# Two last output projections by token tile, with kept weights, and other row statistics

## The chip, the cores and the metric

The kernel runs on 1 core of one Trainium2 chip. The metric is the device time of one execution in microseconds; the time before is 2203.59 us, the median of 3 runs (2201.79 to 2204.91).

## The reference

An encoder trunk of two layers on 512 tokens of width 2048, all float32. Each layer is a mixer with one input projection and one output projection, followed by a residual sum and a layer norm:

```python
for i in range(DEPTH):                          # DEPTH = 2, ALPHA = 4 ** 0.25
    y = attention_mixer(x, ...) if i % 2 == 0 else retention_mixer(x, ...)
    x = layer_norm(ALPHA * x + y, ln_gain[i], ln_bias[i])
```

Layer 0 is grouped-query attention (16 heads of 128 in 4 groups, normalised q and k, rotary positions), its result times a SiLU gate, times `w_out` (2048 x 2048). Layer 1 is retention (8 heads, q and k of 256, v of 512, two directions with decay), each head normalised, times a SiLU gate, times `w_out` (4096 x 2048). `layer_norm` takes mean and variance over the 2048 columns of a token, then gain and bias. Only the second layer norm's result is the output.

## The kernel before, in words

**Numbers.** A float32 product is made of three fp32r matmuls: each operand is split into a high part (a cast on ScalarE, L104) and a low part (a subtraction on VectorE, L105), and `mm3` (L220 to L222) adds high x high, high x low, low x high in one PSUM bank of 128 x 512. So one "product" is three matmuls of 128 x 128 weights and 512 columns.

**Tiles.** The 512 tokens are 4 token tiles of 128 (`t`), the 2048 output columns 4 column blocks of 512 (`c`). Weights come in chunks of 128 x 1024 (512 KB), two pieces of 128 rows x 512 columns each. One list, `order`, holds every chunk of the whole kernel in the order of use; `next_chunk` hands out the next one, has the chunks two further on split (`AHEAD`), and has loads issued three chunks beyond (`FETCH`). Raw chunks lie in pool `rp` (9 buffers), split ones in `wp` (3 buffers each of `whi` and `wlo`). Pool `xp` has 32 buffers of 128 x 1024 (`x4`), used for operands, sums, attention and retention pieces; `tmp` 13 of 128 x 512; PSUM 8 banks.

**Input projections** take one Strassen-like step: seven products (`ORDER`) per block of weights, each with its own "form" of the transposed activations (`Operand.form`), that is a sum or difference of quarters `x11`, `x12`, `x21`, `x22`, split into high and low. Forms 1 and 2 are the quarters of the first two token tiles themselves. `FORMS` says at which chunk of which block's product a form is made; both layers use it.

**Output projections** (`Sum.out_proj`) run once per group of heads, spread between the units of the next group by a `Stream` whose `pump(us)` puts so many us of matmuls (0.68 per product) into PE's order; they add to the residual sum `y` in SBUF (`Sum.add`). The last one of a layer (`out_proj_last`) has no attention or retention beside it. It runs by pairs of token tiles: for the pair `r` = 0, then 2, all four column blocks, so each weight chunk is loaded and split twice (`outs[-1].add(1)` puts a second pass into `order`). After each add, `bn_stats` takes the row statistics of the 512 columns.

**Between the layers**, once a pair of tiles is done, `norm_1` normalises them in place (without gain and bias) and stores them to `nD`; `turn_1` transposes a tile's column block on PE (4 transposes of 128 x 128 into one bank) and writes four pieces of 128 x 128 with gain and bias, two on ScalarE, two on VectorE; for the first pair each is also split at once (128 x 512). Form 5 follows the second pair's turns, and then the hooks make the others.

**At the end**, `norm_2` makes mean and 1 / deviation of a tile (the power on GpSimd, L414), and for each column block subtracts, multiplies by the gain (L926), multiplies by 1 / deviation and adds the bias (L931) on VectorE; the last columns go by ScalarE (L939) and GpSimd (L940, L941). 16 stores go out on SyncE.

**Order.** PE's order is the program's, by hand (`manual_schedule`). The other engines' instructions, DMA queues too, are put in order by a planner that goes by priority (earlier in the program first) among what it holds to be ready and to have a buffer; each engine then runs its list in order.

## Time and profile before

| | |
|---|---|
| median of 3 runs | 2203.59 us |
| profiled execution | 2198.51 us |
| its span | 2196.6 us |
| PE, VectorE, ScalarE, GpSimd busy | 98%, 72%, 48%, 16% |
| mean granted TensorE clock | 0.992 |
| DMA, mean | 165 GB/s |

The span runs from the first to the last instruction; the execution's own time has 1.9 us around it. PE is the matmul engine, PEld its weight load, DVE is VectorE, ACT ScalarE, POOL GpSimd, SP SyncE; SPq is SyncE's queue of DMA issues. The ends of matmuls are modelled: 0.39 us is written for a matmul of 512 columns where the next starts 0.227 us after it. A granted clock of 1.00 is 2.4 GHz.

### The profile page before, as it was taken

Reading aid. Unit: us, or ns where it says so; the run is one execution under the profiler, and the core shown is the slowest. Engines: PE = TensorE matmul, PEld = TensorE weight load, DVE = VectorE, ACT = ScalarE, POOL = GpSimd, SP = SyncE. Lnnn points to the kernel's source line nnn. Section 1 sums busy time; section 2 is a strip of 40 time slices with the busy share of each in tenths; the row PEclk is TensorE's granted clock in tenths of the full one; section 3 lists DMA queues with packets and bytes.
Section 4 is the critical chain, followed back from the end, with each engine's and each line's share of the span. In section 5 each row is a group of like instructions: output and inputs, shape, how many; then the busy total and the mean of one; then the engine's idle time right before and its main releaser. Section 6 shows DMA issues by size and latency. Waiting matters only on the chain.

```text
span 2196.6 us, 26556 instructions
## 1 busy us (share of the span) xinstructions
PE 2142.0 (98%) x9888; PEld 1767.6 (80%) x9888; DVE 1586.9 (72%) x2189; ACT 1043.4 (48%) x1365; POOL 341.5 (16%) x391
## 2 busy tenths in 40 slices
PE   8999999999999999999999999999999999999994
PEld 6778788888888778878888888888888888888883
DVE  6766978887778986767786676657677666666668
ACT  5545446754455654444444444444465333333332
POOL 0322434000000121211212111111111000000004
PEclk9999999999999999999999999999999999999997
DMA  9976666543215688686777558566667433343342
GB/s 337 211 195 133 169 173 148 184 177 106 95 60 171 207 189 220 163 244 177 176 198 210 132 142 213 155 130 183 178 162 262 160 117 107 122 135 125 101 139 77
DMA packets 111600, 361.42 MB, mean 165 GB/s; under 512 B 13680, under 2 KB 17008, under 8 KB 111472
## 3 DMA queue, kind: packets, MB, share of 16 engines
q1 hardware_dynamic: 76272, 235.99, 32.4%
q0 software_dynamic: 35200, 123.75, 25.7%
q8 instruction: 77, 1.26, 0.2%
q14 instruction: 51, 0.42, 0.1%
HBM read 311.45 MB, written 48.23 MB: 164 GB/s over the span
## 4 chain that ended last, share of the span: by engine, by line
PE 82%; DVE 7%; DMA 4%; issue 3%; POOL 2%; ACT 1%; SPq 0%; POOLq 0%; ACTq 0%; DVEq 0%
PE acc L221 23%; PE acc L222 23%; PE acc L220 23%; PE tr L431 3%; DVE wlo L105 3%; DMA raw<-in_wa_in_dram 2%; PE o L220 2%; PE o L222 2%; PE o L221 2%; DMA raw<-in_wr_in_dram 2%; PE s L220 1%; PE s L222 1%; PE s L221 1%; ACT whi L104 1%; DVE f L105 1%
## 5 line engine op out<-in xcount | busy, mean ns | idle before, releaser
L105 DVE TENSOR_TENSOR wlo<-raw,whi 128x1024 fp32r<-128x1024 f32 (+1 forms) x589 | 716.9, 1221 | 362.2 <-ACT whi L104 355.4
L104 ACT CAST whi<-raw 128x1024 fp32r<-128x1024 f32 (+1 forms) x589 | 618.8, 1052 | 744.2 <-PE acc L222 651.4
L220 PE MATMUL acc<-whi,f 128*128 128x512 f32 x1904 | 750.5, 394 | 9.3 <-ACT f L104 4.5
L221 PE MATMUL acc<-wlo,f 128*128 128x512 f32 x1904 | 745.0, 391 | 6.6 <-DVE wlo L105 6.4
L222 PE MATMUL acc<-whi,f 128*128 128x512 f32 x1904 | 743.8, 391 | 0.7 <-DVE f L105 0.7
L221 PEld LDWEIGHTS acc<-wlo,f 128*128 128x128 f32 x1904 | 358.7, 188 | 85.3 <-DVE wlo L105 13.4
L220 PEld LDWEIGHTS acc<-whi,f 128*128 128x128 f32 x1904 | 358.6, 188 | 83.9 <-ACT whi L104 5.2
L222 PEld LDWEIGHTS acc<-whi,f 128*128 128x128 f32 x1904 | 358.3, 188 | 76.7 <-DVE f L105 1.6
L221 PE MATMUL acc<-wlo,ogh 128*128 128x512 f32 x768 | 301.3, 392 | 11.5 <-DVE wlo L105 11.5
L220 PE MATMUL acc<-whi,ogh 128*128 128x512 f32 x768 | 306.0, 398 | 0.5 <-ACT p L604 0.5
L222 PE MATMUL acc<-whi,ogl 128*128 128x512 f32 x768 | 301.0, 392 | 0.0
L221 PEld LDWEIGHTS acc<-wlo,ogh 128*128 128x128 f32 x768 | 145.5, 189 | 40.5 <-DVE wlo L105 12.7
L222 PEld LDWEIGHTS acc<-whi,ogl 128*128 128x128 f32 x768 | 145.2, 189 | 31.1
L220 PEld LDWEIGHTS acc<-whi,ogh 128*128 128x128 f32 x768 | 145.1, 189 | 28.7 <-ACT p L604 0.9
L116 POOL DMA_DIRECT2D raw<-in_wr_in_dram x104 | 91.7, 882 | 384.0 <-DVE wlo L105 246.7
L365 DVE TENSOR_TENSOR y<-acc,y 128x512 f32<-128x512 f32 x176 | 115.6, 684 | 18.7 <-PE acc L222 18.7
L414 POOL TENSOR_TENSOR rstd<-rs_e,neg_half 128x1 f32<-128x1 f32 x40 | 23.8, 597 | 674.4 <-DVE rs_e L413 674.4
L154 DVE TENSOR_TENSOR raw<-raw,raw 128x1024 f32<-128x1024 f32 x52 | 63.5, 1223 | 35.9 <-DMA raw<-in_wr_in_dram 30.9
L152 DVE TENSOR_TENSOR raw<-raw,raw 128x1024 f32<-128x1024 f32 x68 | 82.1, 1218 | 0.8
L328 ACT COPY t<-acc 128x512 f32<-128x512 f32 x102 | 59.0, 587 | 41.9 <-PE acc L222 38.0
L867 ACT ACTIVATE o<-o,nmr,rstd 128x512 f32<-128x512 f32 x32 | 24.9, 779 | 93.4 <-DVE nmr L425 93.4
L604 ACT ACTIVATE p<-s,nmax,q_rs 128x512 f32<-128x512 f32 x64 | 50.0, 781 | 30.6 <-DVE nmax L602 28.2
(159 smaller groups left out, 2098.8 us busy)
## 6 DMA issues: line engine op xcount, KB each, us to landing
raw<-in_wr_in_dram SPq DMA_DIRECT2D x152, 512.0 KB, 4.8
raw<-in_wr_in_dram POOLq DMA_DIRECT2D x104, 512.0 KB, 6.1
raw<-in_wr_o_dram SPq DMA_DIRECT2D x72, 512.0 KB, 3.5
raw<-in_wa_in_dram SPq DMA_DIRECT2D x67, 512.0 KB, 5.1
raw<-in_wa_in_dram POOLq DMA_DIRECT2D x48, 512.0 KB, 6.4
raw<-in_wa_o_dram SPq DMA_DIRECT2D x40, 512.0 KB, 3.5
qkD<-qkT POOLq DMA_DIRECT2D x32, 256.0 KB, 4.4
vDr<-t POOLq DMA_DIRECT2D x32, 256.0 KB, 5.4
```

The source lines that it names most:

```text
L104: nc.scalar.copy(hi, src)
L105: nc.vector.tensor_sub(lo, src, hi.bitcast(F32))
L116: nc.gpsimd.dma_start(out=x, in_=src, accum_op=ALU.add)
L152: nc.vector.tensor_add(v, v, g[3, c])
L154: nc.vector.tensor_add(v, v, g[2, c])
L220: nc.tensor.matmul(ps, sh, mh, start=start, stop=False, skip_group_check=go_on)
L221: nc.tensor.matmul(ps, sh, ml, start=False, stop=False, skip_group_check=go_on)
L222: nc.tensor.matmul(ps, sl, mh, start=False, stop=stop, skip_group_check=go_on)
L328: nc.scalar.copy(keep[p, t], bk[CHAIN[p]][t])
L365: nc.vector.tensor_add(y, ps, y)
L431: nc.tensor.transpose(out=b[:, tcols(i)], in_=src[:, tcols(i)], identity=ident)
L604: nc.scalar.activation(pt, sb, AF.Exp, scale=rs, bias=nmax, accum_out=self.sm[:, h:h + 1])
```

## The change

Both last output projections: the first `A_KEEP` = 2 (attention) or `R_KEEP` = 0 (retention) column blocks go over all four token tiles as in `out_proj`; the others go token tile by token tile, with the split weights of these blocks kept in pool `xp` (8 and 16 buffers), taken up at the first tile. The second pass over the weights is no longer in `order`. Statistics stay `bn_stats` in the first layer (`quick`); in the second the last add also gives a row sum, and ScalarE's squares of the centred row give the variance. `norm_1` and `norm_2` run for each tile. `turn_1` now takes two blocks of 128 columns for both tiles of a pair, transposes four times into one bank and writes two pieces of 128 x 256, one on ScalarE and one on VectorE; forms 1 and 2 are split whole (128 x 1024). Form 7 is made in `x11` instead of `x22`, and forms 3, 7 and 4 are made later, for both layers. `norm_2` is all VectorE but for the squares, with the centred rows in buffers of their own.

```diff
--- before.py
+++ after.py
@@ -33,6 +33,7 @@
 FETCH = 3
 MM3 = 0.68
 LOOK = 2
+A_KEEP, R_KEEP = 2, 0
 ORDER = (1, 5, 6, 3, 7, 2, 4)
 CHAIN = {1: "x", 6: "x", 7: "x", 4: "x", 5: "y", 3: "y", 2: "z"}
@@ -169,16 +170,17 @@
     class Plain:
-        def __init__(self, w):
-            self.w, self.got = w, {}
-        def add(self, half=0):
+        def __init__(self, w, keep=4):
+            self.w, self.got, self.keep = w, {}, keep
+        def add(self):
             for c in range(4):
                 for kc in range(2):
-                    order.append((self, (half, c), kc))
-        def fetch(self, p, kc):
-            self.got[p, kc] = raw_load(self.w[p[1], kc])
+                    order.append((self, c, kc))
+        def fetch(self, c, kc):
+            self.got[c, kc] = raw_load(self.w[c, kc])
         def make(self, p, kc):
             return self.got.pop((p, kc))
@@ -198,7 +200,10 @@
     def make_chunk():
         blk, p, c = order[len(ready)]
         raw = blk.make(p, c)
-        hi, lo = [wp.tile([P, CH], F32R, tag=n, name=nm(n)) for n in ("whi", "wlo")]
+        if isinstance(blk, Plain) and p >= blk.keep:
+            hi, lo = x4("wkh"), x4("wkl")
+        else:
+            hi, lo = [wp.tile([P, CH], F32R, tag=n, name=nm(n)) for n in ("whi", "wlo")]
         split(hi, lo, raw)
         blk.follow(p, c)
         ready.append([(half(hi, j), half(lo, j)) for j in range(2)])
@@ -268,9 +273,9 @@
             elif n == 3:
                 nc.vector.tensor_add(x12, x12, x11)
             elif n == 7:
-                nc.vector.scalar_tensor_tensor(out=x22, in0=x11, scalar=-1.0, in1=x22,
+                nc.vector.scalar_tensor_tensor(out=x11, in0=x11, scalar=-1.0, in1=x22,
                                                op0=ALU.mult, op1=ALU.subtract)
-            split(*self.new_form(n, i), {1: x11, 2: x12, 5: x21, 6: x11, 4: x22, 3: x12, 7: x22}[n])
+            split(*self.new_form(n, i), {1: x11, 2: x12, 5: x21, 6: x11, 4: x22, 3: x12, 7: x11}[n])
         def st(self, n, k, t):
             return [m[:, k % 4, tcols(t)] for m in self.f[n, k // 4]]
@@ -345,8 +350,9 @@
     class Sum:
-        def __init__(self):
-            self.y, self.st, self.rows = {}, {}, []
+        def __init__(self, quick=()):
+            self.y, self.st, self.rows, self.quick = {}, {}, [], quick
         def load(self, src):
             for t in range(NT):
@@ -357,16 +363,23 @@
                         self.y[t, 2 * i + j] = half(m, j)
                     self.y[t, "pair", i] = m
-        def add(self, t, c, ps, scale):
+        def add(self, t, c, ps, scale, last=False):
             y = self.y[t, c]
-            if scale != 1.0:
+            if last and t not in self.st:
+                self.st[t] = small("ln_st", 24)
+            if last and t not in self.quick:
+                nc.vector.scalar_tensor_tensor(out=y, in0=y, scalar=scale, in1=ps, op0=ALU.mult, op1=ALU.add,
+                                               accum_out=self.st[t][:, c:c + 1])
+            elif scale != 1.0:
                 nc.vector.scalar_tensor_tensor(out=y, in0=y, scalar=scale, in1=ps, op0=ALU.mult, op1=ALU.add)
             else:
                 nc.vector.tensor_add(y, ps, y)
-        def out_proj(self, og, scale):
-            for c in range(4):
+            if last and t in self.quick:
+                nc.vector.bn_stats(self.st[t][:, 6 * c:6 * c + 6], y)
+        def out_proj(self, og, scale, cols=(0, 1, 2, 3), last=False):
+            for c in cols:
                 banks = {}
                 for kc in range(2):
                     ks = next_chunk()
@@ -379,28 +392,36 @@
                             mm3(banks[t], og(k, t), ks[kk], k == 0, k == 3)
                             yield MM3
                 for t in range(NT):
-                    self.add(t, c, banks[t], scale)
-        def out_proj_last(self, og):
...
-                self.rows.append(r)
+                    self.add(t, c, banks[t], scale, last)
+        def mean_rstd(self, t):
+            if t in self.quick:
+                return mean_rstd(self.st[t])
+            mu, neg, sq, rstd = small("k_rs", 4)[:, 0:1], small("nmr"), small("sm", 4), small("rstd")
+            nc.vector.tensor_reduce(out=mu, in_=self.st[t][:, :4], axis=AX.X, op=ALU.add)
+            nc.vector.tensor_scalar_mul(neg, mu, -1.0 / D)
+            nc.vector.tensor_scalar_mul(mu, mu, 1.0 / D)
+            for c in range(4):
+                nc.scalar.activation(temp("sq"), self.y[t, c], AF.Square, bias=neg, accum_out=sq[:, c:c + 1])
+            nc.vector.tensor_reduce(out=neg, in_=sq, axis=AX.X, op=ALU.add)
+            rsqrt(rstd, neg, 1.0 / D, LN_EPS)
+            return mu, rstd
+        def out_proj_last(self, og, keep):
+            yield from self.out_proj(og, 1.0, range(keep), True)
+            ws = {}
+            for t in range(NT):
+                for c in range(keep, 4):
+                    b = bank()
+                    for k in range(4):
+                        if t == 0 and k % 2 == 0:
+                            ws[c, k // 2] = next_chunk()
+                        mm3(b, og(k, t), ws[c, k // 2][k % 2], k == 0, k == 3)
+                        yield MM3
+                    self.add(t, c, b, 1.0, True)
+                self.rows.append(t)
     ident = const.tile([P, P], F32, name="ident")
@@ -434,8 +455,8 @@
     a_in = [Block(a["wa_in"][g], g < 2) for g in range(A_G)]
     r_in = [Block(a["wr_in"][g], g < 2) for g in range(R_G)]
-    a_out = [Plain(a["wa_o"][g]) for g in range(GROUPS)]
-    r_out = [Plain(a["wr_o"][h]) for h in range(R_HEADS)]
+    a_out = [Plain(a["wa_o"][g], A_KEEP if g == GROUPS - 1 else 4) for g in range(GROUPS)]
+    r_out = [Plain(a["wr_o"][h], R_KEEP if h == R_HEADS - 1 else 4) for h in range(R_HEADS)]
     for ins, outs in ((a_in, a_out), (r_in, r_out)):
         for b in ins[:2]:
             b.add((1, 2))
@@ -445,7 +466,6 @@
             b.add(ORDER)
         for b in outs:
             b.add()
-        outs[-1].add(1)
     def in_stream(ins, op, evacuate, n):
@@ -456,8 +476,8 @@
         for b in ins[2:len(ins) - n]:
             yield from products(b, op, ORDER, evacuate)
-    FORMS = (((1, 2, 1), (6, 0)), ((1, 2, 3), (6, 1)), ((0, 5, 0), (4, 0)), ((0, 5, 1), (4, 1)),
-             ((0, 5, 2), (3, 0)), ((0, 5, 3), (3, 1)), ((0, 6, 0), (7, 0)), ((0, 6, 1), (7, 1)))
+    FORMS = (((1, 2, 1), (6, 0)), ((1, 2, 3), (6, 1)), ((0, 5, 1), (3, 0)), ((0, 5, 3), (3, 1)),
+             ((0, 3, 0), (7, 0)), ((0, 3, 2), (7, 1)), ((0, 7, 0), (4, 0)), ((0, 7, 2), (4, 1)))
     def form_hooks(ins, op):
         for (b, p, c), what in FORMS:
@@ -671,7 +691,7 @@
     ev1 = spill(deliver_1)
     Stream(in_stream(a_in, x1, ev1, 1)).drain()
     groups = [Group(g) for g in range(GROUPS)]
-    total = Sum()
+    total = Sum(range(NT))
     work = Stream(products(a_in[-1], x1, ORDER, ev1))
     work.pump(31.5 * MM3)
     groups[0].load_kv()
@@ -724,7 +744,7 @@
     x2 = Operand()
     def norm_1(t):
-        mu, rstd = mean_rstd(total.st[t])
+        mu, rstd = total.mean_rstd(t)
         scale, shift = scale_shift(mu, rstd)
         for c in (0, 2, 1, 3):
             y = total.y[t, c]
@@ -735,22 +755,24 @@
         for i in range(2):
             nc.gpsimd.dma_start(out=nD[:, t, i * 1024:i * 1024 + 1024], in_=total.y[t, "pair", i])
-    def turn_1(t, c):
-        b = transpose4(total.y[t, c])
...
-                                     scale=lnt[:, 0, k:k + 1], bias=lnt[:, 1, k:k + 1])
+    def turn_1(r, m):
+        b = bank("tr")
+        kh, i = m // 4, m // 2 % 2
+        for k in (2 * m, 2 * m + 1):
+            for t in range(2):
+                nc.tensor.transpose(out=b[:, tcols(k % 2 * 2 + t)],
+                                    in_=total.y[2 * r + t, k // 4][:, tcols(k % 4)], identity=ident)
+        for k in (2 * m, 2 * m + 1):
+            o = 256 * (k % 2)
+            f = x2.quarter(r, kh, i)[:, k % 4]
+            if k % 2:
+                nc.vector.tensor_scalar(f, b[:, o:o + 256], lnt[:, 0, k:k + 1], lnt[:, 1, k:k + 1],
+                                        op0=ALU.mult, op1=ALU.add)
             else:
-                nc.vector.tensor_scalar(f[:, j], b[:, tcols(j)], lnt[:, 0, k:k + 1], lnt[:, 1, k:k + 1],
-                                        op0=ALU.mult, op1=ALU.add)
-        if r == 0:
-            if (1 + kh, i) not in x2.f:
-                x2.new_form(1 + kh, i)
-            split(*[m[:, :, cols] for m in x2.f[1 + kh, i]], f)
+                nc.scalar.activation(f, b[:, o:o + 256], AF.Identity, scale=lnt[:, 0, k:k + 1], bias=lnt[:, 1, k:k + 1])
+        if r == 0 and m % 2:
+            x2.form(1 + kh, i)
     def residual_2(c, t, gb={}):
@@ -916,56 +938,29 @@
                 lnp[-1] += [half(u, j) for j in range(2)]
     def norm_2(t):
-        mu, rstd = mean_rstd(total.st[t])
-        def store(c):
-            nc.sync.dma_start(out=out[t, :, c * 512:c * 512 + 512], in_=total.y[t, c])
-        def centre(c):
+        mu, rstd = total.mean_rstd(t)
+        z = [half(m, j) for m in (x4("z", F32), x4("z", F32)) for j in range(2)] if t > 1 else [temp("z") for _ in range(4)]
+        for c in range(4):
             y = total.y[t, c]
-            return nc.vector.scalar_tensor_tensor(out=y, in0=y, scalar=mu, in1=lnp[0][c],
-                                                  op0=ALU.subtract, op1=ALU.mult)
-        def finish(c):
+            nc.vector.scalar_tensor_tensor(out=z[c], in0=y, scalar=mu, in1=lnp[0][c], op0=ALU.subtract, op1=ALU.mult)
+        for c in range(4):
             y = total.y[t, c]
-            nc.vector.scalar_tensor_tensor(out=y, in0=y, scalar=rstd, in1=lnp[1][c], op0=ALU.mult, op1=ALU.add)
-            store(c)
...
-            finish(c)
+            nc.vector.scalar_tensor_tensor(out=y, in0=z[c], scalar=rstd, in1=lnp[1][c], op0=ALU.mult, op1=ALU.add)
+            nc.sync.dma_start(out=out[t, :, c * 512:c * 512 + 512], in_=y)
     ev2 = spill(deliver_2)
-    work = Stream(total.out_proj_last(groups[-1].out), in_stream(r_in, x2, ev2, 1))
-    work.until(lambda: 0 in total.rows)
...
-        x2.form(5, h)
+    work = Stream(total.out_proj_last(groups[-1].out, A_KEEP), in_stream(r_in, x2, ev2, 1))
+    for r in range(2):
+        for t in (2 * r, 2 * r + 1):
+            work.until(lambda: t in total.rows)
+            norm_1(t)
+        work.pump(13.0 if r else 5.0)
+        for m in (0, 1, 4, 5, 2, 3, 6, 7) if r else range(8):
+            turn_1(r, m)
+            work.pump(2.2 if r else 0.8)
+            if r and m in (5, 7):
+                x2.form(5, m // 2 % 2)
     form_hooks(r_in, x2)
     work.drain()
@@ -983,15 +978,12 @@
         work.drain()
         if h == 0:
             total.load(lambda t: yD2[:, t])
-    work = Stream(total.out_proj_last(heads[-1].out))
-    work.pump(20.0)
+    work = Stream(total.out_proj_last(heads[-1].out, R_KEEP))
+    work.pump(5.0)
     ln_params()
-    work.until(lambda: 0 in total.rows)
-    norm_2(0)
-    norm_2(1)
-    work.drain()
-    norm_2(2)
-    norm_2(3)
+    for t in range(NT):
+        work.until(lambda: t in total.rows)
+        norm_2(t)
```

## Rows read from the trace of the kernel before

**Rows 1.** The page's first line and PE's busy time (share of the span, instructions).

```profile
span 2196.6 us, 26556 instructions
PE 2142.0 (98%) x9888; PEld 1767.6 (80%) x9888; DVE 1586.9 (72%) x2189; ACT 1043.4 (48%) x1365; POOL 341.5 (16%) x391
```

**Rows 2.** The timeline of PE in the last output projection: start, duration, engine, line, operation, output and inputs, and in brackets the idle time before and what ended it.

```profile
2151.91 0.39 PE L220 MATMUL acc<-whi,ogh 128*128 128x512 f32 x1
2160.78 0.80 PE L221 MATMUL acc<-wlo,ogh 128*128 128x512 f32 x1 [8.48 <-DVE wlo L105]
...
2165.18 0.40 PE L222 MATMUL acc<-whi,ogl 128*128 128x512 f32 x1
```

**Rows 3.** The timelines of PE and of VectorE at the end, the last row of each.

```profile
2176.55 0.39 PE L222 MATMUL acc<-whi,ogl 128*128 128x512 f32 x1
...
2192.63 0.75 DVE L931 SCALAR_TENSOR_TENSOR y<-y,rstd,ln_bias 128x512 f32<-128x512 f32 x1
```

**Rows 4.** The timeline of PE between the layers.

```profile
716.88 0.39 PE L220 MATMUL acc<-whi,ogh 128*128 128x512 f32 x1
720.09 0.50 PE L221 MATMUL acc<-wlo,ogh 128*128 128x512 f32 x1 [2.83 <-DVE wlo L105]
...
724.79 0.39 PE L222 MATMUL acc<-whi,ogl 128*128 128x512 f32 x1
...
734.80 0.66 PE L431 MATMUL tr<-ident,y 128*128 128x128 f32 x4 [1.24 <-DVE y L732]
...
794.71 0.50 PE L220 MATMUL acc<-whi,f 128*128 128x512 f32 x1 [0.32 <-ACT whi L104]
796.98 0.50 PE L221 MATMUL acc<-wlo,f 128*128 128x512 f32 x1 [1.77 <-DVE wlo L105]
```

**Rows 5.** The timeline of PE in the first layer's input projection.

```profile
76.32 0.39 PE L220 MATMUL acc<-whi,f 128*128 128x512 f32 x1
78.01 0.50 PE L221 MATMUL acc<-wlo,f 128*128 128x512 f32 x1 [1.31 <-DVE wlo L105]
```

**Rows 6.** Busy time of each engine in stretches (start:end and length, then PE, PEld, DVE, ACT, POOL with instructions in brackets, granted clock, DMA share, GB/s).

```profile
55.00:79.00 24.00, 22.69 (x100) 18.50 (x99) 23.57 (x22) 15.39 (x17) 5.35 (x7) 1.00 0.88 193
...
699.00:728.00 29.00, 25.99 (x121) 20.35 (x120) 28.10 (x54) 20.78 (x36) 3.66 (x6) 0.94 0.53 187
728.00:775.00 47.00, 45.76 (x222) 37.65 (x221) 45.04 (x71) 32.94 (x48) 8.83 (x12) 1.00 0.87 260
775.00:800.00 25.00, 22.91 (x104) 18.57 (x103) 25.00 (x32) 12.67 (x16) 5.56 (x7) 1.00 0.56 126
800.00:830.00 30.00, 29.63 (x131) 24.22 (x130) 18.28 (x18) 13.37 (x14) 8.79 (x12) 1.00 1.01 242
...
2161.30:2164.70 3.40, 3.40 (x9) 2.67 (x8) 3.40 (x5) 0.00 (x0) 2.16 (x2) 0.50 0.09 33
```

**Rows 7.** The timelines of VectorE and GpSimd around that stop of PE, in order of time.

```profile
2148.64 0.74 DVE L931 SCALAR_TENSOR_TENSOR y<-y,rstd,ln_bias 128x512 f32<-128x512 f32 x1
2149.30 0.74 DVE L926 SCALAR_TENSOR_TENSOR y<-y,mv,ln_gain 128x512 f32<-128x512 f32 x1
...
2152.85 1.71 POOL L940 TENSOR_TENSOR y<-y,ln_gain 128x512 f32<-128x512 f32 x1
2154.52 0.54 POOL L414 TENSOR_TENSOR rstd<-rs_e,neg_half 128x1 f32<-128x1 f32 x1
2155.09 0.21 DVE L425 TENSOR_SCALAR nmr<-mv,rstd 128x1 f32<-128x1 f32 x1 [1.66 <-POOL rstd L414]
...
2158.44 2.28 DVE L105 TENSOR_TENSOR wlo<-raw,whi 128x1024 fp32r<-128x1024 f32 x1
```

**Rows 8.** Groups of instructions by line and shape on VectorE and ScalarE, over the whole run: busy us and mean ns of one, then the idle time before them and what ended it.

```profile
L105 DVE TENSOR_TENSOR wlo<-raw,whi 128x1024 fp32r<-128x1024 f32 x587 | 715.5, 1222 | 358.8 <-ACT whi L104 352.1 <-DMA ln_bias<-in_ln_bias_dram 2.0 <-DMA xf<-in_xq_dram 1.7
...
L402 DVE BATCH_NORM_STATS2 ln_st<-y 128x6 f32<-128x512 f32 x32 | 20.5, 677 | 0.0
L748 DVE TENSOR_SCALAR xf<-tr,lnt 128x128 f32<-128x128 f32 x32 | 11.2, 402 | 0.7 <-ACT xf L745 0.6
L363 DVE SCALAR_TENSOR_TENSOR y<-y,acc 128x512 f32<-128x512 f32 x16 | 10.6, 680 | 2.4 <-PE acc L222 2.4
L413 DVE TENSOR_SCALAR rs_e<-mv 128x1 f32<-128x1 f32 x40 | 6.0, 151 | 1.1
...
L104 ACT CAST whi<-raw 128x1024 fp32r<-128x1024 f32 x587 | 617.5, 1053 | 742.7 <-PE acc L222 651.4 <-DMA raw<-in_wr_in_dram 20.7 <-issue 17.0
L604 ACT ACTIVATE p<-s,nmax,q_rs 128x512 f32<-128x512 f32 x64 | 50.0, 781 | 30.6 <-DVE nmax L602 28.2 <-issue 1.2 <-PE tr L431 0.7
L604 ACT ACTIVATION_READ_ACCUMULATOR p<-s,nmax,q_rs 128x1 f32 x64 | 12.5, 195 | 0.0
```

**Rows 9.** The timeline of ScalarE: one exponential with its accumulator's read.

```profile
660.15 0.78 ACT L604 ACTIVATE p<-s,nmax,q_rs 128x512 f32<-128x512 f32 x1
660.82 0.20 ACT L604 ACTIVATION_READ_ACCUMULATOR p<-s,nmax,q_rs 128x1 f32 x1
```

**Rows 10.** The timeline of SyncE's queue around the start of the last output projection (start, stretch of the merged issues, line, destination and source).

```profile
2107.42 0.33 SPq L112 DMA_DIRECT2D raw<-in_wr_o_dram  x1
2107.84 0.86 SPq L915 DMA_DIRECT2D ln_gain<-in_ln_gain_dram  x2
...
2119.13 17.40 SPq L112 DMA_DIRECT2D raw<-in_wr_o_dram  x6
```

More of the change, by code (lines that the diff above doesn't have):

```diff
@@ L381, in out_proj @@
                 for t in range(NT):
-                    self.add(t, c, banks[t], scale)
-        def out_proj_last(self, og):
-            for r in (0, 2):
-                for c in range(4):
-                    banks = {}
-                    for kc in range(2):
-                        ks = next_chunk()
-                        for kk in range(2):
-                            k = kc * 2 + kk
-                            for t in (r, r + 1):
-                                if k == 0:
-                                    banks[t] = bank()
-                                mm3(banks[t], og(k, t), ks[kk], k == 0, k == 3)
-                                yield MM3
-                    for t in (r, r + 1):
-                        self.add(t, c, banks[t], 1.0)
-                        if c == 0:
-                            self.st[t] = small("ln_st", 24)
-                        nc.vector.bn_stats(self.st[t][:, 6 * c:6 * c + 6], self.y[t, c])
-                self.rows.append(r)
+                    self.add(t, c, banks[t], scale, last)
@@ L929, in finish @@
-        def finish(c):
+            nc.vector.scalar_tensor_tensor(out=z[c], in0=y, scalar=mu, in1=lnp[0][c], op0=ALU.subtract, op1=ALU.mult)
+        for c in range(4):
             y = total.y[t, c]
-            nc.vector.scalar_tensor_tensor(out=y, in0=y, scalar=rstd, in1=lnp[1][c], op0=ALU.mult, op1=ALU.add)
-            store(c)
-        own = 2 if t < NT - 1 else 3
-        centre(0)
-        scale, shift = scale_shift(mu, rstd)
-        for c in range(own, 4):
-            y = total.y[t, c]
-            nc.scalar.activation(y, y, AF.Identity, scale=scale, bias=shift)
-            nc.gpsimd.tensor_mul(y, y, lnp[0][c])
-            nc.gpsimd.tensor_add(y, y, lnp[1][c])
-            store(c)
@@ L943, in norm_2 @@
-        finish(0)
-        for c in range(1, own):
-            tc.keep_in_program_order(centre(c))
-            finish(c)
-    ev2 = spill(deliver_2)
-    work = Stream(total.out_proj_last(groups[-1].out), in_stream(r_in, x2, ev2, 1))
-    work.until(lambda: 0 in total.rows)
-    norm_1(0)
-    norm_1(1)
-    work.pump(4.0)
-    for t in range(2):
-        for c in (0, 1, 2, 3):
-            turn_1(t, c)
-            work.pump(1.2)
-    work.until(lambda: 2 in total.rows)
-    norm_1(2)
-    norm_1(3)
@@ L962, in encoder_trunk_kernel @@
-    work.pump(5.0)
-    for h in range(2):
-        for t in (2, 3):
-            for c in (h, h + 2):
-                turn_1(t, c)
-                work.pump(1.2)
-        x2.form(5, h)
+            nc.vector.scalar_tensor_tensor(out=y, in0=z[c], scalar=rstd, in1=lnp[1][c], op0=ALU.mult, op1=ALU.add)
+            nc.sync.dma_start(out=out[t, :, c * 512:c * 512 + 512], in_=y)
+    ev2 = spill(deliver_2)
+    work = Stream(total.out_proj_last(groups[-1].out, A_KEEP), in_stream(r_in, x2, ev2, 1))
```

6 lines of the change are left out of this document (removed).

## The prediction

> **What bounds the kernel now.** I read the page first: the span is 2196.6 us and PE is busy for 98% of it [rows 1]. So the matmul stream is the bound, and a change that leaves the number of matmuls alone can gain only where PE stands still, where its clock has fallen, or after its last matmul. A busy figure hides such places (ends are modelled), so I read PE's starts in order of time. In a full stretch they are 0.227 us apart. The waits of PE and the gaps in its starts lie in few places:
>
> - At the end of the kernel. Between the starts 2151.91 and 2160.78 nothing runs, 8.64 us more than a step; then ten steps take 4.40 us where 2.27 are usual, at a granted clock of 0.50 (1.2 instead of 2.4 GHz) after 8.7 us without matmuls, so 2.13 us are lost again [rows 2, 6]. That is 10.8 us.
> - After PE. The last matmul ends at 2176.55 + 0.39 = 2176.94; the span goes on for 19.66 us, with VectorE, ScalarE and GpSimd taking turns, the last vector instruction ending at 2193.38 and the last store 3.2 us behind it [rows 3].
> - At the border of the layers. PE waits at 720.09 (2.98 over a step) and runs 13 steps in 4.70 instead of 2.95 us behind it (1.75 lost, the slow step of the end again), then stands for 1.24 at 734.80, 0.32 at 794.71 and 2.04 over a step at 796.98 [rows 4]: 8.3 us.
> - In the first layer at 78.01, 1.46 us, in a stretch where VectorE is busy for 23.57 of 24 us [rows 5, 6].
>
> Why they come is in VectorE's rows. From 699 to 800 us it is busy for 98.1 of 101 us, against 61% in the 30 us behind that [rows 6], and PE's waits there are for the low halves of weights (L105) and for the normalised `y` [rows 4]. At the end, the split of a weight chunk (2158.44) stands in VectorE's queue behind the finish of tile 1, which waits for a power on GpSimd, which in turn stands behind GpSimd's multiplications [rows 7].
>
> **The change, part by part.** The matmuls (64 products of three each in either projection) and the transposes (64) stay the same in number.
>
> *The second pass over the weights goes.* Each last projection took 16 chunks and takes 8. Per layer that removes eight loads, eight casts of 1.053 and eight subtractions of 1.222 us [rows 8]: 9.8 us of VectorE. At the end this takes away the very instruction that PE waited for: nothing that PE needs is any longer behind the normalisation. PE then waits for VectorE only where a bank has to come free, with eight banks, 21.8 us of matmuls. Of the 10.8 us I count 10.3, leaving 0.5 for small waits in the first token tile, where 8 chunks are used in 10.9 us: VectorE needs 8 x 1.222 + 4 x 0.68 = 12.5 us for them, but the kept chunks have slots of their own and need not wait for PE. Of its 16 loads only the last six are issued from 2119.13 on, while it begins at about 2122 (its 192 matmuls of 0.227 and the 10.8 us lost, counted back from PE's end) [rows 2, 3, 10]: with 8 instead of 16, all is on the chip before the start. Bounds: 10.8 if the splits are done ahead; if they keep program order, 2.7 us of adds come first and 1.8 us of clock follow a wait, 6 us gained.
>
> *The end.* Behind the last matmul now stand one token tile's last add, its statistics and its normalisation. From rows: an add that scales, out of PSUM, 0.68; the accumulator's read, which VectorE does not show here, between 0 and the 0.195 of ScalarE's, taken as 0.2; a sum over four and two small products, 0.5 by the 0.15 of such a one; four squares with accumulators, each 0.67 to the next instruction and 0.195 for the read as with the exponentials, 3.5, and 0.1 to get there; sum, scale, power on GpSimd (0.54) and hand-offs 1.3; four finishes of 0.75, starting 0.66 apart, 2.7; and the 3.2 of the last store [rows 3, 7 to 9]. Together 12.2 us, against 19.66: 7.4 gained. The four centrings (4 x 0.75) lie beside ScalarE's squares and cost nothing; without that cover they would cost up to 3.0. The tile before it ends its last add 10.9 us earlier and needs some 9 us after that, so only its last finishes could touch this chain, up to 2. Bounds: 9 and 2.4.
>
> VectorE's accumulating form is not in this trace. The Trainium skill ("VectorE: DVE Perf Modes", Two Vector instructions with no wait between them) says that an op which also writes out its accumulator is two instructions, so sixteen more in VectorE's queue and one on the end path; with it the end path has the 0.2 counted above, without it 12.0. A rule that speaks against the new end is in the skill's "Vector Engine (DVE) Microarchitecture Reference", Points that are easy to get wrong: a scalar_tensor_tensor with two SBUF sources that are not bf16 runs at half throughput. The row of the finish, which is such an instruction, is 0.75 us for 512 columns [rows 3], beside 0.68 with one source in PSUM [rows 8], so the trace does not bear it out; half throughput beyond the row would put some 4 x 0.5 us on the end path and the gain would be 23.0 instead of 25.0 in all.
>
> *Moved loads and queues.* `ln_params` moves from 20 to 5 us into the projection. Its loads were issued from 2107.84 on, before the projection begins [rows 10]: a free buffer decides, not the place in the program. With 16 buffers of kept weights, 8 of `y`, 4 of outputs and these 4, all 32 of the pool are held; the third and fourth tile's two buffers for the centred rows must wait until a kept chunk is done with, which the first products of the fourth tile do 1.4 us in. Cost 0; late parameters would be covered by the 10.9 us of the first tile. In the middle, the two `nD` stores of each tile now stand in GpSimd's queue ahead of the next tile's power. They wait for the normalised row, some 4 us behind a tile's last matmul; the next power is wanted some 7 us behind it. Cost 0, below nothing excluded; beyond 3 us of lateness it would hold the next tile.
>
> *The border.* VectorE's turns become 16 of 256 columns instead of 32 of 128: 11.2 us [rows 8] become 8.0 at 0.5 each. No row has this form; its bounds are 0.402 (128 columns) and 0.684 (512, from PSUM), and I take a value nearer to the former, with ScalarE alike. The splits of forms 1 and 2, 8 of 0.68 before, are 4 of 1.22, the same. Forms 7 and 4 (6 vector instructions, about 6.6 us) leave the stretch up to 800 for the two products behind it, where VectorE has 39% free. So 98.1 - 9.8 - 3.2 - 6.6 = 78.5 us of work stand in a stretch of about 94: 83%, not 97%. The 1.24 at 734.80 has its own remedy: 13 instead of 5 us of matmuls ahead of the second turns. What is late next: behind the second column block VectorE has 4 adds and 4 statistics (5.4 us) in one burst while PE wants a kept chunk every 1.36 us, and the first product of the next layer needs two turns and a wide split. I put 2.0 us on that, so 8.3 - 2.0 = 6.3 gained. Bounds: 8.3, and below nothing, -10, where each of the first four chunks or forms comes a burst late and the clock falls.
>
> *The forms in the first layer.* The same reordering thins the stretch at 55 to 79; of 1.46 I count 1.0. Bounds 1.5 and, as a later form could be late for its product, -1.5.
>
> **Sum:** 10.3 + 7.4 + 6.3 + 1.0 = 25.0 us. The profiled execution took 2198.51 us (1.9 around its span), so it would be 2173.5. The median of the timed runs lies 5.1 above the profiled one; from it, 2203.6 - 25.0 = 2178.6.
>
> **The rivals.**
> 1. *The splits are not done ahead, or the border stays bound by VectorE.* For it: VectorE's 97%, and that every cast of weights begins behind PE's release (651 of ScalarE's 743 us of waiting there) [rows 8], which shows no run-ahead of ScalarE. Against: those casts have three buffers, and SyncE's loads do run far ahead of the program [rows 10]. Then the border gains nothing and the end 4 less: 25.0 - 6.3 - 4 = 14.7, so 2189; with one of the two 2183 to 2185.
> 2. *Slower: VectorE's queue meets the turns too early.* If the sixteen turns stand in its in-order queue ahead of splits, it waits for PE's transposes, which come 0.8 or 2.2 us of matmuls apart: up to 8 x 0.8 + 8 x 2.2 = 24 us of idle VectorE where 94 - 78.5 = 15.5 are free. 8.5 us of lateness would cost PE about 13 with its clock, by 2.98 and 1.75 [rows 4]; with the border's 6.3 not gained and a second burst in the first products the same again, 26 lost against 18.7, 2211. It decides from 19 us lost at the border on. Against: before, the turns stood 1.2 us apart, and VectorE's 32 turns waited 0.7 us in all, for ScalarE and not for PE [rows 8].
> 3. *Only the end path improves, the matmul stream doesn't:* kept chunks come late, PE's stops move to the first token tile, 25.0 - 10.3 - 6.3 - 1 = 7.4, 2196. For it only the 12.5 against 10.9 us.
>
> **How the numbers follow.** My forecast (gain 20 to 33) has 0.65, rival 1 0.20, rival 3 0.05, rival 2 0.06, a difference too small to tell 0.04. A measurement of this kernel tells 0.2%, 4.4 us, from no change. Faster 0.90, within 0.2% 0.04, slower 0.06. Range: down to 2168, where every bound is reached on the good side (10.8 + 9 + 8.3 + 1.5 = 29.6, and 5 for the profiled run's shorter time), and up to 2190, rival 1 whole.
>
> **What would show it.** In the profile after: no gap of PE over 1 us in its last 43.5 us and a granted clock of 1.00 there; 11 to 14 us from the last matmul to the end, with four squares on ScalarE in it and none of GpSimd's multiplications; casts of kept chunks in 2105 to 2121 ahead of PE; VectorE near 83% at the border and less than 3 us of waits of PE there; 16 chunk loads fewer. I am wrong if PE waits for L105 in the first token tile (rival 1 or 3), if VectorE waits for transposes with weights queued behind (rival 2), or if the end path is over 15 us.

## The result and the profile after

The changed kernel took 2178.07 us (median; 2176.01 to 2178.84) beside 2204.11 for the kernel before: ratio 0.9886, 95% interval 0.9873 to 0.9899, 25 us faster. The forecast was 2178.6.

The profiled executions tell less: 2178.59 us after, 2198.51 before, 19.9 apart. Timed runs of the kernel before spread from 2198.4 to 2209.2 us over all the comparisons below, so its profiled one was a short one. One execution of the kernel before took 5585 us and is left out of every time here. The terms below are read from profiles and checked by timed runs.

Page of the changed kernel, first line and busy times, beside [rows 1]:

```profile
span 2176.8 us, 26428 instructions
PE 2140.8 (98%) x9888; PEld 1767.4 (81%) x9888; DVE 1557.8 (72%) x2175; ACT 1028.9 (47%) x1354; POOL 319.6 (15%) x377
```

Shares have hardly moved. What moved is seen in stretches (columns as in [rows 6]):

```profile
55.00:79.00 24.00, 24.00 (x106) 19.56 (x105) 22.06 (x21) 16.89 (x19) 5.92 (x8) 1.00 0.91 198
699.00:728.00 29.00, 29.00 (x146) 24.15 (x145) 24.60 (x48) 12.37 (x19) 5.62 (x10) 1.00 0.34 127
728.00:775.00 47.00, 47.00 (x229) 38.93 (x227) 41.35 (x55) 30.92 (x39) 7.02 (x9) 1.00 0.80 228
775.00:800.00 25.00, 21.04 (x82) 16.40 (x81) 23.31 (x30) 10.74 (x14) 5.88 (x7) 0.86 0.56 109
...
2121.50:2165.40 43.90, 43.90 (x195) 36.16 (x193) 31.49 (x73) 9.92 (x26) 2.37 (x3) 1.00 0.20 72
```

The last projection runs without a stop at a granted clock of 1.00. The border starts better (146 matmul instructions, transposes among them, from 699 to 728, not 121) and ends worse (82 from 775 to 800, not 104, at a clock of 0.86).

PE's lost time, stretch by stretch, is what its starts exceed 0.227 us after a matmul and 0.11 after a transpose, where that is over 0.02 us, summed from the timelines of PE; the end path runs from the last matmul's end to the end of the span. All in us:

| kernel | 0-100 | 100-640 | 640-770 | 770-830 | 830-2080 | from 2080 | end path | span |
|---|---|---|---|---|---|---|---|---|
| before | 10.8 | 16.6 | 8.8 | 3.4 | 10.8 | 11.6 | 19.7 | 2196.6 |
| before, again | 10.7 | 14.9 | 8.8 | 5.0 | 12.9 | 11.8 | 19.7 | 2199.1 |
| changed | 10.9 | 16.5 | 2.9 | 8.4 | 11.3 | 0.4 | 11.2 | 2176.8 |
| changed, again | 10.2 | 17.7 | 3.0 | 7.1 | 11.2 | 0.4 | 11.3 | 2176.2 |
| end_only | 10.6 | 16.6 | 8.8 | 5.0 | 12.7 | 0.4 | 11.4 | 2180.5 |
| border_only | 10.8 | 17.8 | 3.0 | 5.5 | 11.0 | 11.6 | 19.6 | 2194.3 |
| pairs_newnorm | 11.8 | 16.4 | 2.9 | 7.1 | 11.8 | 9.9 | 16.9 | 2191.9 |
| tiles_oldnorm | 11.0 | 17.1 | 3.0 | 7.1 | 9.8 | 0.4 | 12.0 | 2175.3 |
| quick3 | 10.2 | 18.0 | 3.0 | 5.4 | 10.8 | 0.4 | 10.6 | 2173.7 |
| forms_old | 10.7 | 16.3 | 2.9 | 9.9 | 9.2 | 0.4 | 11.3 | 2175.6 |
| turns_old | 11.2 | 17.2 | 3.5 | 9.2 | 12.3 | 0.4 | 11.3 | 2180.1 |
| pump5 | 11.5 | 17.1 | 3.1 | 1.4 | 10.1 | 0.4 | 11.2 | 2170.1 |
| dma_p6 | 10.0 | 18.4 | 3.0 | 1.1 | 10.0 | 0.4 | 11.3 | 2169.2 |
| dma_p6_quick3 | 10.2 | 18.9 | 3.0 | 1.1 | 10.4 | 0.4 | 10.5 | 2169.3 |

Between the profiles of the first and third row the end gives 11.2 + 8.4 = 19.6 us, nearly all of the 19.8 by which the spans differ; the border gives 5.9 and takes 5.0 back. From 100 to 640 us, where little of the change acts, the runs differ by up to 4.0 us (14.9 to 18.9).

Why nothing stops PE at the end: the timeline of VectorE shows six of the eight kept chunks split before the projection begins (at 2121.9), between the last head's work, where [rows 10] had shown only the loads running ahead:

```profile
2111.74 4.62 DVE L106 TENSOR_TENSOR wkl<-raw,wkh 128x1024 fp32r<-128x1024 f32 x4
...
2116.88 2.35 DVE L106 TENSOR_TENSOR wkl<-raw,wkh 128x1024 fp32r<-128x1024 f32 x2
```

The end path, from the same timeline with PE's last row ahead, beside [rows 3]:

```profile
2165.18 0.39 PE L227 MATMUL acc<-wkh,ogl 128*128 128x512 f32 x1
...
2165.61 0.69 DVE L371 SCALAR_TENSOR_TENSOR y<-y,acc 128x512 f32<-128x512 f32 x1 [1.31 <-PE acc L227]
2166.22 0.08 DVE L371 DVE_READ_ACCUMULATOR y<-y,acc 128x1 f32 x1
2166.34 0.16 DVE L402 TENSOR_REDUCE k_rs<-ln_st 128x1 f32<-128x4 f32 x1
...
2166.91 2.74 DVE L945 SCALAR_TENSOR_TENSOR z<-y,k_rs,ln_gain 128x512 f32<-128x512 f32 x4
2169.68 0.16 DVE L407 TENSOR_REDUCE nmr<-sm 128x1 f32<-128x4 f32 x1
...
2170.75 2.74 DVE L948 SCALAR_TENSOR_TENSOR y<-z,rstd,ln_bias 128x512 f32<-128x512 f32 x4 [0.72 <-POOL rstd L435]
```

Four centrings (2166.91 to 2169.65) fit beside ScalarE's squares, whose sum VectorE takes up at 2169.68. Where the border's gain goes is in PE's timeline, the changed kernel's answer to [rows 4]:

```profile
784.70 0.50 PE L226 MATMUL acc<-wlo,f 128*128 128x512 f32 x1 [1.59 <-DVE wlo L106]
...
791.25 0.50 PE L225 MATMUL acc<-whi,f 128*128 128x512 f32 x1 [0.60 <-ACT whi L105]
793.52 0.79 PE L226 MATMUL acc<-wlo,f 128*128 128x512 f32 x1 [1.77 <-DVE wlo L106]
794.12 0.63 PE L227 MATMUL acc<-whi,f 128*128 128x512 f32 x1
794.54 0.63 PE L225 MATMUL acc<-whi,f 128*128 128x512 f32 x1
```

The stops at 720.09 and 734.80 of before are gone; those at 794.71 and 796.98 are there at 791.25 and 793.52, one at 784.70 is new, and behind the last the steps are 0.43 us for six microseconds.

### The profile page after: what moved, and what is told of

Read it like the earlier page. It is cut to its first block, busy times and chain, and to the rows that moved or that the text cites. A ratio compares the mean times of both kernels' runs of the same rounds, so it can differ in the third digit from the quotient of the medians.

```text
span 2176.8 us, 26428 instructions
## 1 busy us (share of the span) xinstructions
PE 2140.8 (98%) x9888; PEld 1767.4 (81%) x9888; DVE 1557.8 (72%) x2175; ACT 1028.9 (47%) x1354; POOL 319.6 (15%) x377
## 4 chain that ended last, share of the span: by engine, by line
PE 85%; DVE 6%; DMA 5%; issue 2%; ACT 1%; POOL 0%; SPq 0%; DVEq 0%; POOLq 0%; ACTq 0%
PE acc L226 24%; PE acc L225 24%; PE acc L227 24%; PE tr L452 3%; DVE wlo L106 3%; DMA raw<-in_wa_in_dram 2%; PE o L225 2%; PE o L227 2%; PE o L226 2%; DMA raw<-in_wr_in_dram 2%; PE s L225 1%; PE s L227 1%; PE s L226 1%; ACT whi L105 1%; DVE f L106 0%
## 5 line engine op out<-in xcount | busy, mean ns | idle before, releaser
L106 DVE TENSOR_TENSOR wlo<-raw,whi 128x1024 fp32r<-128x1024 f32 (+1 forms) x561 | 682.4, 1220 | 365.9 <-ACT whi L105 359.9
L105 ACT CAST whi<-raw 128x1024 fp32r<-128x1024 f32 (+1 forms) x561 | 588.8, 1051 | 711.4 <-PE acc L227 616.9
L225 PE MATMUL acc<-whi,f 128*128 128x512 f32 x1904 | 751.4, 395 | 10.3 <-ACT f L105 4.8
L225 PE MATMUL acc<-whi,ogh 128*128 128x512 f32 x672 | 266.6, 397 | 0.6 <-ACT ogh L105 0.4
L227 PE MATMUL acc<-whi,ogl 128*128 128x512 f32 x672 | 262.4, 391 | 0.0
L226 PE MATMUL acc<-wlo,ogh 128*128 128x512 f32 x672 | 262.0, 390 | 0.0
L227 PEld LDWEIGHTS acc<-whi,ogl 128*128 128x128 f32 x672 | 126.1, 188 | 27.5 <-DVE ogl L106 0.4
L225 PEld LDWEIGHTS acc<-whi,ogh 128*128 128x128 f32 x672 | 126.3, 188 | 25.4 <-ACT ogh L105 0.8
L226 PEld LDWEIGHTS acc<-wlo,ogh 128*128 128x128 f32 x672 | 126.5, 188 | 24.0
L376 DVE TENSOR_TENSOR y<-acc,y 128x512 f32<-128x512 f32 x160 | 105.7, 685 | 17.6 <-PE acc L227 17.6
```

Source lines behind the costliest of these rows:

```text
L105: nc.scalar.copy(hi, src)
L106: nc.vector.tensor_sub(lo, src, hi.bitcast(F32))
L225: nc.tensor.matmul(ps, sh, mh, start=start, stop=False, skip_group_check=go_on)
L226: nc.tensor.matmul(ps, sh, ml, start=False, stop=False, skip_group_check=go_on)
L227: nc.tensor.matmul(ps, sl, mh, start=False, stop=stop, skip_group_check=go_on)
L376: nc.vector.tensor_add(y, ps, y)
```

## The experiments

Theory E, formed from the two profiles: only the end pays. Its rival is the prediction's sum, in which border and forms pay 7.3. The first four runs set them against each other and ask how far one profile can be trusted.

**Both kernels once more.**

> The kernel before, once more, with a profile. In the two profiles the spans differ by 19.8 us, in the timed medians by 26.0. Theory A (the profiled execution of before was a lucky one): a second profile shows a span about 2200 to 2203, and the extra 4 to 6 us lie in stops of PE between 640 and 830 or behind 2121. Theory B (a profiled execution of this kernel is always shorter than a timed one): span again 2196 to 2198 and timed again 2202 to 2205. Ratio 1.000 in either.

> The changed kernel, once more. Ratio 0.9885, 25 us. Theory A: its profiled span lies again within 2 us of 2176.8, since its matmul stream has fewer stops that can come out longer or shorter. Theory B: likewise, but then the timed gain would stay 5 us above the profiled one.

Measured: before 0.9998 (0.9987 to 1.0009), span 2199.1; changed 0.9872 (0.9858 to 0.9886), span 2176.2. Neither theory as put: the second profile lies 2.5 us above the first and still below the timed median (2201.0 against 2202.4). It loses 1.6 us more from 770 to 830 and 2.1 more behind 830, but 1.7 less from 100 to 640. One profile of this kernel is good to some 3 us, not to 1.

**One layer's part at a time.** In end_only the first layer's code is that of before; in border_only the second's is. First end_only's main lines, then border_only's:

```diff
...
-    a_out = [Plain(a["wa_o"][g], A_KEEP if g == GROUPS - 1 else 4) for g in range(GROUPS)]
+    a_out = [Plain(a["wa_o"][g], 4) for g in range(GROUPS)]
...
-    work = Stream(total.out_proj_last(groups[-1].out, A_KEEP), in_stream(r_in, x2, ev2, 1))
+    work = Stream(total.out_proj_pairs(groups[-1].out), in_stream(r_in, x2, ev2, 1))
...
```

```diff
...
-    work = Stream(total.out_proj_last(heads[-1].out, R_KEEP))
-    work.pump(5.0)
+    work = Stream(total.out_proj_pairs(heads[-1].out))
+    work.pump(20.0)
...
```

> Only the second layer's part of the change: token tiles and kept weights at the end, the new norm_2 and its row statistics; the border of the layers, its turns and the forms are those of before. Theory E (the end alone pays; border and forms come out at nothing): 19 to 20 us by the profiles, ratio 0.989 to 0.991, the same as the whole change within 2 us. The prediction's sum: 17.7 us of 25.0, so 7 us slower than the whole change.

> Only the first layer's part: token tiles and kept weights there, the new turns, and the forms made later; the end is that of before, with its pairs, its second pass and its norm_2. Theory E: within 2 us of the kernel before (ratio 0.999 to 1.001), PE some 4 to 5 us ahead at 770 us and level again at 800. The prediction's sum: 7.3 us faster, ratio 0.9967.

Measured: end_only 0.9904 (0.9891 to 0.9917), 21.2 us; border_only 0.9966 (0.9954 to 0.9978), 7.5 us, 4.8 to 10.1. Theory E falls: its 0.999 to 1.001 lies outside the second interval, and end_only is 7 us behind the whole change, as the sum has it, though its 21.2 (18.3 to 24.0) lies above the 17.7 counted for it. The two parts add up to 28.7 where the whole, timed beside them, gave 28.2. The lost times say how: 640 to 770 falls from 8.8 to between 2.9 and 3.5 in every run with the new border, and 770 to 830 is 0.5 to 5.0 higher in border_only and the changed kernel's two profiles than in those of before. By profile border_only is only 2.3 to 4.8 us ahead (2194.3 against 2196.6 and 2199.1); where the rest of the 7.5 us by time lies, these profiles don't show.

**What makes the end.** pairs_newnorm takes the order of before with the new norm_2, tiles_oldnorm the new order with norm_2 and the statistics of before, quick3 batch statistics for the last tile (the edit shown).

```diff
-    total = Sum()
+    total = Sum((3,))
```

> The changed kernel, but the last output projection of the second layer runs by pairs of token tiles and takes its weights twice, as before; norm_2, its statistics and the first layer's part are the new ones. Theory S (PE stopped for 8.64 us at the end because the second pass's splits stand in VectorE's queue behind a normalisation, whichever): a stop of PE of 5 us or more in the last projection, and 15 to 18 us from the last matmul to the end, since two tiles are normalised there. Rival G (the stop was GpSimd's, whose multiplications held up the power): below 3 us of stops, as GpSimd has none of them any more.

> The changed kernel with kept weights and token tiles at the end, but with norm_2 and the row statistics of before (GpSimd's multiplications too). Theory S: PE stops for less than 1 us in its last 43.5 us, and the end path is 10 to 12 us, no longer than with the new norm_2 (11.2): the order of the tiles makes the gain. Rival N (the new norm_2 shortens the end path by taking GpSimd out of it): 14 us or more from the last matmul to the end.

> The changed kernel with the row statistics of before (batch statistics on VectorE) for the last token tile of the second layer alone. Four squares with their reads stand on the end path now (2.95 us), but the four centrings (2.74 us) beside them: the end path falls by 0.5 to 1.2 us, from 11.2 to about 10.3. If the squares cost what they last, by 2 us or more.

Measured by profile: pairs_newnorm stops PE for 7.21 us (lost 9.9 in all) and has an end path of 16.9; theory S holds and G falls, for GpSimd has no multiplication in it and the stop is there all the same. PE's timeline there, then VectorE's:

```profile
2151.62 0.39 PE L225 MATMUL acc<-whi,ogh 128*128 128x512 f32 x1
2159.06 0.79 PE L226 MATMUL acc<-wlo,ogh 128*128 128x512 f32 x1 [7.05 <-DVE wlo L106]
```

```profile
2155.14 2.73 DVE L969 SCALAR_TENSOR_TENSOR y<-z,rstd,ln_bias 128x512 f32<-128x512 f32 x4
2157.79 1.22 DVE L106 TENSOR_TENSOR wlo<-raw,whi 128x1024 fp32r<-128x1024 f32 x1
```

The split that PE wants stands behind the finishes of tile 1, as in [rows 7], whoever makes the normalisation. tiles_oldnorm loses 0.4 us and ends in 12.0, 0.8 longer than with the new norm_2 where no difference was expected; rival N falls. PE runs through there too, with GpSimd at work (columns as above):

```profile
2119.20:2162.90 43.70, 43.70 (x195) 36.16 (x193) 34.53 (x55) 5.67 (x8) 20.06 (x15) 1.00 0.18 66
```

So the order of the tiles takes away PE's stop, and most of the end path's 8.4 us. How much of these is the order's depends on what comes first: on top of the old norm_2 it gives 7.7 (19.7 to 12.0) and the new norm_2 then 0.8; on top of the new norm_2 it gives 5.7 (16.9 to 11.2), after 2.8 from the norm_2. quick3 ends in 10.6, 0.6 less: without the squares, the batch statistics and the four centrings lie on the path themselves.

**The forms** where they were made before, and form 7 in x22 (that edit is not shown):

```diff
...
-    FORMS = (((1, 2, 1), (6, 0)), ((1, 2, 3), (6, 1)), ((0, 5, 1), (3, 0)), ((0, 5, 3), (3, 1)),
-             ((0, 3, 0), (7, 0)), ((0, 3, 2), (7, 1)), ((0, 7, 0), (4, 0)), ((0, 7, 2), (4, 1)))
+    FORMS = (((1, 2, 1), (6, 0)), ((1, 2, 3), (6, 1)), ((0, 5, 0), (4, 0)), ((0, 5, 1), (4, 1)),
+             ((0, 5, 2), (3, 0)), ((0, 5, 3), (3, 1)), ((0, 6, 0), (7, 0)), ((0, 6, 1), (7, 1)))
```

> The changed kernel with the forms made where and as before (4, 3 and 7 during the first block's fifth and sixth product, 7 in x22), in both layers. Theory V (from 775 to 800 VectorE's own load sets PE's pace, and the forms only shift it): PE's lost time from 0 to 100 us 10 to 11 as with either kernel, from 770 to 830 between 5 and 9, ratio to before 0.986 to 0.989. The prediction's term for the first layer: 1 us slower than the changed kernel.

Measured: 0.9902 (0.9886 to 0.9919), lost time 10.7 from 0 to 100, as theory V has it, and 9.9 from 770 to 830, above its 5 to 9. In the first layer the stop of before is back and the changed kernel's are gone; PE's timeline in forms_old, then in the changed kernel:

```profile
78.00 0.50 PE L226 MATMUL acc<-wlo,f 128*128 128x512 f32 x1 [1.31 <-DVE wlo L106]
```

```profile
96.38 0.50 PE L225 MATMUL acc<-whi,f 128*128 128x512 f32 x1 [0.85 <-ACT whi L105]
97.64 0.50 PE L226 MATMUL acc<-wlo,f 128*128 128x512 f32 x1 [0.76 <-DVE wlo L106]
101.30 0.50 PE L226 MATMUL acc<-wlo,f 128*128 128x512 f32 x1 [0.61 <-DVE wlo L106]
```

So the forms only shift the first layer's stop. Whether they help by time stays open: the ratio is above the forecast, but its interval meets both of the changed kernel's (0.9873 to 0.9899 and 0.9858 to 0.9886).

**The border: turns and cushion.** turns_old puts the narrow turns back at the new places; pump5 takes 8 us of matmuls from ahead of the second pair's turns.

```diff
-        work.pump(13.0 if r else 5.0)
+        work.pump(5.0)
```

> The changed kernel with the turns of before (a tile's four 128 x 128 pieces, narrow splits for the first pair) at the same places. If the wider turns matter by the 3 us of VectorE that they save: a stop of PE of 1 to 3 us between 700 and 770, where the changed kernel has none. If the second pass over the weights was all: lost time from 640 to 770 stays at 3 us.

> The changed kernel with 5 instead of 13 us of matmuls ahead of the second pair's turns. The prediction's step (the 1.24 us wait of before at 734.80 is cured by the 13 us): PE waits 1 to 1.5 us for the normalised y near 730. If the token tiles cured it (the fourth tile alone is late, not two): below 0.5 us.

Measured: turns_old has no stop of PE from 700 to 770 (lost 3.5 from 640 on), so the narrow turns alone did not make the stop at 720.09. PE waited there for a split of the second pass, which is gone in both; that this alone is the cure was not tested apart. Its 770 to 830 is 9.2, at the upper end of the others. pump5 has no wait for the normalised `y` at all, and it loses only 1.4 us from 770 to 830, with a span of 2170.1. Its stretches show why, against the changed kernel's above:

```profile
728.00:775.00 47.00, 47.00 (x228) 38.88 (x227) 45.05 (x58) 32.61 (x41) 7.38 (x10) 1.00 0.76 225
775.00:800.00 25.00, 24.66 (x113) 20.19 (x112) 24.32 (x31) 15.04 (x18) 6.71 (x8) 1.00 0.69 127
```

VectorE is busy for 45.05 of the 47 us behind 728 instead of 41.35. In the changed kernel it stands idle there five times, waiting for ScalarE's casts of weights, and these wait for PE, as the waits in this stretch say. The reading is that the weights' three buffers forbid to split further ahead while the turns have not come yet:

```profile
ACT whi L105 <- PE acc L227: 7.0, 6, 2.1
DVE wlo L106 <- ACT whi L105: 5.6, 5, 1.5
```

The turns and the forms behind them then fall later, the forms on the stretch from 775 on. pump5 ran once only (2171.91 us; the changed kernel's eight runs, in other sessions, took 2173.04 to 2178.84). But three stops of about 1.74, 0.76 and 2.04 us are in all six profiles so far with the new border, its turns, its forms and the 13 us, and here only one of 0.60 is left.

**The load itself.** In the first two blocks the sixth product's weights are the sum of three quarters; VectorE adds the third, 1.22 us a chunk. Here a DMA adds it:

```diff
-            if p == 6:
+            if p == 6 and not self.first:
                 nc.vector.tensor_add(v, v, g[3, c])
...
             elif p == 6 and self.first:
                 onto(g["v", c], q(21))
+            elif p == 5 and self.first:
+                onto(g["v", c], q(22))
```

> The changed kernel, but in the first two blocks of either input projection the sum for the sixth product (the quarter 22 onto the sum of 11 and 12) is made by an accumulating DMA into the raw chunk instead of by VectorE: eight additions of 1.22 us fewer per layer, 4 more loads of 512 KB per block. Theory V (PE's stops at 785 to 794, and those at 60 to 102 in the first layer, come from VectorE's own load in the stretch where each chunk costs it an addition and a subtraction, 2.4 us against 2.72 us of matmuls): these stops fall from 4.5 to below 1.5 us, lost time from 770 to 830 from 7 to 8 down to 4 or less, ratio to before 0.983 to 0.986 (the changed kernel: 0.987 to 0.989). Rival P (the planner puts a form's operation ahead of a chunk's wherever the load is): the stops stay within 1 us. Rival D: the sums come late, and casts wait for DMA.

> The same with batch statistics for the last token tile. Theory V: 0.6 us less than dma_p6 by the profile, ratio 0.983 to 0.986, the fastest of all. Rivals as there.

Measured: dma_p6 0.9863 (0.9846 to 0.9879), lost time 1.1 from 770 to 830 and no stop above 0.54 us there, span 2169.2; with batch statistics for the last tile 0.9858 (0.9843 to 0.9873), span 2169.3, where 0.6 less than dma_p6 was expected. dma_p6 from 775 to 800, and what its casts of weights wait for from 770 to 830:

```profile
775.00:800.00 25.00, 24.93 (x115) 20.42 (x114) 23.69 (x31) 16.60 (x20) 9.07 (x12) 1.00 1.04 200
```

```profile
ACT whi L105 <- DMA raw<-in_wr_in_dram: 12.6, 6, 2.7
```

Theory V holds for the border, and rival P falls. Rival D's waits are there, six casts that wait 12.6 us for DMA in all where the changed kernel's first profile has none; but PE does not stop for them. In the first layer the stops at 96 to 101 go, while others of 0.5 to 0.9 from 60 to 77 stay or vary: its lost time is 10.0 and 10.2, as in the changed kernel, so theory V is not shown there. Of the ratios 0.9863 just misses the forecast's 0.983 to 0.986 and 0.9858 lies in it, and their intervals meet the changed kernel's: by profile some 7 us, by time not told apart.

## Why the prediction was right, and where it was not

The end came as forecast and better. The stop and its slow steps: 10.3 counted; from 2080 us on 11.2 of 11.6 went, as the first token tile costs nothing when splits run ahead. The end path: 12.2 counted, 11.2 found. Its terms: the add 0.69 (0.68), the accumulator's read 0.08 (0.2), the squares 2.94 in all (3.6), the finishes 2.74 (2.7). The accumulating add is two instructions, as the Trainium skill says ("VectorE: DVE Perf Modes", Two Vector instructions with no wait between them), the second of 82 ns on average. Half throughput for two SBUF sources is not seen in the changed kernel: 16 centrings took 747 ns on average, where this add with one source in PSUM took 684.

The 0.75 us that the prediction took for a finish is its price without GpSimd's multiplications beside it, which the prediction did not say. In the kernel before, 10 of the 18 such instructions of the last normalisation took 1.62 to 1.76 us: just those that start while GpSimd multiplies or adds (L940, L941). The other eight took 0.74 to 0.75, as did all 32 of the changed kernel:

```profile
2151.28 1.60 POOL L941 TENSOR_TENSOR y<-y,ln_bias 128x512 f32<-128x512 f32 x1
2151.67 1.76 DVE L931 SCALAR_TENSOR_TENSOR y<-y,rstd,ln_bias 128x512 f32<-128x512 f32 x1
```

The border came out at the forecast size by time (7.5 with the forms, 7.3 counted), but not by its steps, which give 0.9 us between the first two profiles and 3.7 between the second two where 6.3 were counted. Of the lost time from 640 to 770, 5.9 us went, nearly what 720.09 and 734.80 had cost (2.98 + 1.75 + 1.24). The prediction then let the stops behind 790 go too, for two reasons that fell. "Forms 7 and 4 ... leave the stretch up to 800": VectorE's timeline of the changed kernel has both of form 7's operations inside it, where they had stood at 793.44 and 799.11 before. The planner takes them when it holds their inputs to be ready; the hook's place is only a priority. First the kernel before, then the changed one:

```profile
793.44 1.21 DVE L271 SCALAR_TENSOR_TENSOR xf<-xf,xf 128x1024 f32<-128x1024 f32 x1
...
799.11 1.21 DVE L271 SCALAR_TENSOR_TENSOR xf<-xf,xf 128x1024 f32<-128x1024 f32 x1
```

```profile
791.12 1.22 DVE L276 SCALAR_TENSOR_TENSOR xf<-xf,xf 128x1024 f32<-128x1024 f32 x1
792.26 3.48 DVE L106 TENSOR_TENSOR wlo<-raw,whi 128x1024 fp32r<-128x1024 f32 x3
...
796.80 1.21 DVE L276 SCALAR_TENSOR_TENSOR xf<-xf,xf 128x1024 f32<-128x1024 f32 x1
```

And "The 1.24 at 734.80 has its own remedy: 13 instead of 5 us": pump5 shows that the wait stays away without the 13 us, and that these leave VectorE idle early and overloaded later. The prediction's load was also too small. From 699 to 800 VectorE's busy time fell from 98.1 to 89.3 us (24.60 + 41.35 + 23.31), by 8.9, where 19.6 were counted: six weight splits fewer stand there and not eight (24 instead of 30), and of the 6.6 us of forms 7 and 4 only form 4's two splits left. And the sum over 94 us, 83% busy, hid where the load lies: 41.35 of 47 and 23.31 of 25 are 88% and 93%, with waits in the one and a queue in the other.

The turns were sized right (0.539 us each where 0.5 was taken from bounds of 0.402 and 0.684), but without that saving PE does not stop from 700 to 770 either (turns_old). The first layer's 1.0 us did not come: 10.8 and 10.7 us lost before, 10.9 and 10.2 after.

Rival 1 was half right: the border's second half stayed bound by VectorE, but splits were done ahead. One sign that the prediction named for itself, less than 3 us of waits of PE at the border, failed: 1.59 + 0.60 + 1.77 = 3.96 us from 784 to 794. Rival 2 looked for VectorE waiting for turns that come too early; they came too late. Rival 3 did not occur.

That the total fits so well, 2178.6 against 2178.07, is partly fortune. By profile, on which the sum was built, the gain is 19.9 us between the first two and 23.1 between the second two, not 25.0; the end's better terms make up for part of the border's worse ones. By time it is 25 to 28 us. Carrying the sum over to the timed median of 2203.6 assumed that every run would be 5.1 above its profile, and the changed kernel's are not (2178.59 profiled, 2178.07 median). Both profiles of before were short ones of their kind; where the longer executions lose their time no profile shows.

## What to carry to other kernels

Look for a second pass over data whose preparation stands in an in-order queue behind something slow, as here behind a normalisation; keep the prepared data, and the order of the tiles can then be chosen so that only one tile's epilogue lies behind the last matmul. A busy share over a long stretch does not show that an engine waits in its first half for work that overloads it in the second: cut the stretch where the load changes, and look at what moves early work late, even a cushion meant to remove a wait. One profile is one draw: part of what it shows may be its own, so time both halves of a change before saying which pays.

## What the runs showed of the hardware

The same stops of PE can cost more in one execution than in another. Those of 1.74, 0.76 and 2.04 us from 784 to 794 are, within 0.04 us and shifted by up to a microsecond, in six profiles with the same code in this stretch, and behind them the granted clock differed. From 794 to 800, in the changed kernel's profile, its second one and quick3's:

```profile
794.00:800.00 6.00, 6.00 (x16) 4.60 (x16) 4.31 (x5) 1.90 (x3) 2.50 (x3) 0.52 0.80 145
```

```profile
794.00:800.00 6.00, 5.87 (x19) 4.71 (x20) 5.51 (x6) 3.10 (x4) 2.62 (x3) 0.72 0.86 164
```

```profile
794.00:800.00 6.00, 5.75 (x25) 4.79 (x26) 6.00 (x7) 3.54 (x5) 2.62 (x3) 1.00 0.78 150
```

16, 19 and 25 matmul instructions in six microseconds; the lost time from 770 to 830 was 8.4, 7.1 and 5.4 us. In the first, the steps of 0.43 us are those of the lower clock of 1.2 GHz. What decides it did not show in these traces.
